# A feed-forward layer computed in two phases, most of its matrix products in two by two blocks with seven block products in place of eight

## The chip, the core and the metric

The kernel runs on one core of a Trainium2 chip. Its engines are TensorE (PE, matrix products into the accumulation memory PSUM), VectorE (DVE), ScalarE (ACT), GpSimd (POOL) and SyncE (SP), whose queue here issues every transfer between the device memory and the on-chip memory SBUF. Each engine works through its own list of instructions in order and waits at an instruction until what it needs is there. The metric is the device time of one execution in microseconds (us).

## The reference

One layer of a streaming encoder on 1024 new frames and 32 frames of a running stream, together T = 1056 rows of width D = 1024, all in float32. What matters here is the end of the layer, the feed-forward part:

```
mix = einsum(g_conv * y_conv + g_attn * y_attn, w_o)
x1  = layer_norm(ALPHA * x + mix)                         # LN1
h   = square(relu(einsum('btd,df->btf', x1, w_up)))       # 1024 -> 4096
out = layer_norm(ALPHA * x1 + einsum('btf,fd->btd', h, w_down))   # 4096 -> 1024, LN2
```

Before it stand an input projection, a convolution branch and an attention branch; the change does not touch them. The outputs also hold the keys, values and gate logs, which are unaffected.

## The kernel before

**Number format.** Every float32 operand of a product is split into a high and a low part (`whi`, `wlo` of a weight, `x1_0h`, `x1_0l` of an activation), and a product is the sum of three passes: high by high, high by low, low by high. So one block of 128 inputs by 128 outputs by n rows is three matmuls, each with its own load of 128x128 weights and n columns that stream through. `mm3` writes these passes and `dense` runs them to the end. A split is a copy on ACT (the high part) and a subtraction on DVE or POOL (the low part).

**Tiling.** Activations lie transposed: 128 channels on the partitions, the 1056 rows along the free axis. The rows are cut into three chunks of 352. Weights come as tiles of 128 outputs by 1024 inputs through the class `Weights`: `load` fetches half a tile (256 KB) into one of four `raw` buffers, `split` makes the high and low parts in a ring of four (`RB`), `take` and `drop` hand them out. From line 724 on the low parts of the weights are made on POOL (`W.engine = "pool"`).

**Order.** PE, DVE, ACT and POOL run exactly in the order in which the kernel's code records instructions; the class `Issue` records them and keeps a rough clock for each engine to decide when a background piece (a weight split, a step of a normalisation) is put in between. SP's order is set by the framework's scheduler.

**Merge, output projection, LN1.** The merge (`ps_yc`, `ps_yo`) works on 24 pieces of 128 channels by 352 rows. Then, chunk after chunk, `ps_o` is formed with `w_o` and added to the input into `acc` (eight tiles of 128x1056); `norm_out` runs LN1 as a background piece, whose `emit` writes the split `x1` tiles that the feed-forward part reads, and leaves `x1` itself in `acc`.

**Feed-forward.** An outer loop over eight blocks `fb` of four tiles of 128 hidden channels (`FB` = 4, `NFB` = 8). In each block `up` forms four tiles of hidden channels (8 input tiles x 3 passes = 24 matmuls of 352 columns for each tile and chunk); ACT takes the relu out of PSUM, DVE squares it (`r`), copies the high part (`hh`) and subtracts (`hl`). Then `down` forms the partial sums of eight output tiles (12 matmuls for each tile and chunk), and DVE adds each to `acc`. Hidden tiles never leave SBUF. In the last block the rows are handled in three pieces so that LN2 of an earlier piece runs beside the products of a later one; the end is written out by hand after LN2 of the last piece.

## Time and profile before

| | |
|---|---|
| Median of three runs | 1547.46 us (1547.21 to 1547.95) |
| Profiled execution, its own time | 1548.1 us |
| Its span from first to last instruction | 1546.3 us |
| Granted TensorE clock, mean | 0.988 |
| PE busy | 1501.4 us, 9524 matmuls |
| DVE, ACT, POOL busy | 900.7, 500.8, 466.5 us |
| Bytes moved | 165.57 MB, 107 GB/s over the span |
| Merge and output projection | about 600 to 773 us |
| Feed-forward with LN2 | about 773 us to the end |

How to read it: a group's row gives the source line (that of a helper such as `mm`, L205), the engine, the operation, the tile written and the tiles read, the shape and the count, then busy time, the mean duration of one instruction in ns, and the idle time of its engine just before, with what ended it. A matmul's own duration is much longer than its share of time, because matmuls overlap; the distance from one start to the next is what counts. A row of a stretch gives its length, each engine's busy time and (x count), the granted clock of TensorE (1.00 is full), the busy share of the 16 transfer engines and the rate in GB/s.

### The profile page before, as it was taken

The page shows a single profiled execution, that of the slowest core. Times are in us where ns is not written, and L with a number is a line of the kernel's source. Part 1 is how long each engine was busy: PE and PEld are TensorE (multiplying, and loading weights), DVE is VectorE, ACT ScalarE, POOL GpSimd, SP SyncE. Part 2 cuts the span into 40 slices and gives each one's busy share as a digit, 9 for nine tenths or more (in the row PEclk, how much of TensorE's full clock was granted, in tenths as well). Part 3 has the DMA queues.
Part 4 walks back from the last instruction along what each step waited for, and adds up shares of the span by engine and source line. Part 5 has one row for each costly group of instructions (what it writes and reads, how often), then busy time and mean ns, then how long its engine had stood idle before and what let it go on. Part 6 is the DMA issues. An engine that isn't in the chain of part 4 may idle for free.

```text
span 1546.3 us, 24721 instructions
## 1 busy us (share of the span) xinstructions
PE 1501.4 (97%) x9524; PEld 1473.8 (95%) x9524; DVE 900.7 (58%) x1461; ACT 500.8 (32%) x1086; POOL 466.5 (30%) x439
## 2 busy tenths in 40 slices
PE   9999999989999999999899999999999999999985
PEld 8999999989999998999899999999999999999984
DVE  6999899746666656748784342433334243342587
ACT  5123432536555564236541111211111021111133
POOL 0000000003454534567844222222222122231346
PEclk9999999999999999999999999999999999999998
DMA  6125453376445666544412111111111111114312
GB/s 232 43 77 160 165 175 126 131 215 168 134 129 169 171 225 207 153 139 146 142 42 81 42 42 55 42 42 55 42 42 55 42 42 55 42 59 146 137 38 75
DMA packets 114115, 165.57 MB, mean 107 GB/s; under 512 B 19530, under 2 KB 72010, under 8 KB 113998
## 3 DMA queue, kind: packets, MB, share of 16 engines
q1 hardware_dynamic: 113998, 163.99, 34.4%
q8 instruction: 75, 1.23, 0.3%
q14 instruction: 42, 0.34, 0.1%
HBM read 120.38 MB, written 43.54 MB: 106 GB/s over the span
## 4 chain that ended last, share of the span: by engine, by line
PE 83%; DVE 8%; DMA 3%; issue 2%; ACT 2%; SPq 1%; POOL 1%; ACTq 0%; DVEq 0%; POOLq 0%
PE ps_dn L205 22%; PE ps_up L205 22%; PE ps_g L205 9%; PE ps_v L205 3%; PE ps_glub L205 3%; PE ps_k L205 3%; PE ps_glua L205 3%; PE ps_q L205 3%; PE ps_o L205 2%; PE ps_s L205 2%; PE ps_pv L205 2%; PE ps_yc L205 2%; PE ps_tr L209 2%; DVE acc L234 2%; PE ps_yo L205 2%
## 5 line engine op out<-in xcount | busy, mean ns | idle before, releaser
L226 POOL TENSOR_TENSOR wlo<-raw,whi 128x512 fp32r<-128x512 f32 x204 | 285.6, 1421 | 542.4 <-ACT whi L217 541.3
L217 ACT ACTIVATE whi<-raw 128x512 fp32r<-128x512 f32 (+1 forms) x264 | 152.0, 623 | 405.4 <-issue 317.7
L205 PE MATMUL ps_dn<-hh,whi 128*128 128x352 f32 x768 | 249.4, 325 | 0.0
L205 PE MATMUL ps_dn<-hl,whi 128*128 128x352 f32 x768 | 247.8, 323 | 0.8 <-DVE hl L226 0.8
L205 PE MATMUL ps_dn<-hh,wlo 128*128 128x352 f32 x768 | 248.0, 323 | 0.0
L226 DVE TENSOR_TENSOR acc<-ps_dn,acc 128x352 f32<-128x352 f32 x168 | 87.8, 523 | 194.5 <-PE ps_dn L205 194.5
L234 DVE SCALAR_TENSOR_TENSOR ca<-u,prm,ca 128x1086 f32<-128x1086 f32 x120 | 161.7, 1348 | 2.4
L226 DVE TENSOR_TENSOR r<-r 128x352 f32<-128x352 f32 x96 | 52.5, 547 | 184.7 <-ACT r L217 184.7
L205 PEld LDWEIGHTS ps_dn<-hl,whi 128*128 128x128 f32 x768 | 144.5, 188 | 1.3 <-DVE hl L226 1.0
L205 PEld LDWEIGHTS ps_dn<-hh,whi 128*128 128x128 f32 x768 | 144.3, 188 | 0.6 <-DVE acc L226 0.2
L205 PEld LDWEIGHTS ps_dn<-hh,wlo 128*128 128x128 f32 x768 | 144.4, 188 | 0.0
L205 PE MATMUL ps_g<-xh,whi 128*128 128x352 f32 x384 | 132.4, 345 | 6.3 <-ACT gt L217 6.3
L217 ACT ACTIVATE r<-ps_up 128x352 f32<-128x352 f32 x96 | 44.5, 464 | 260.0 <-PE ps_up L205 253.5
L205 PE MATMUL ps_g<-xh,wlo 128*128 128x352 f32 x384 | 124.1, 323 | 0.0
L205 PE MATMUL ps_g<-xl,whi 128*128 128x352 f32 x384 | 122.0, 323 | 0.0
L226 DVE TENSOR_TENSOR hl<-r,hh 128x352 fp32r<-128x352 f32 x96 | 84.8, 883 | 3.3
L226 DVE TENSOR_TENSOR tl<-ps_tr,th 128x512 fp32r<-128x512 f32 (+2 forms) x96 | 51.2, 553 | 58.3 <-ACT th L217 57.5
L205 PE MATMUL ps_up<-x_0h,whi 128*128 128x352 f32 x256 | 82.9, 324 | 0.0
L205 PE MATMUL ps_up<-x_1h,wlo 128*128 128x352 f32 x256 | 82.4, 322 | 0.0
L205 PE MATMUL ps_up<-x_0h,wlo 128*128 128x352 f32 x256 | 82.4, 322 | 0.0
L205 PE MATMUL ps_up<-x_1h,whi 128*128 128x352 f32 x256 | 82.4, 322 | 0.0
L205 PE MATMUL ps_up<-x_0l,whi 128*128 128x352 f32 x256 | 82.3, 322 | 0.0
(281 smaller groups left out, 3774.9 us busy)
## 6 DMA issues: line engine op xcount, KB each, us to landing
raw<-in_w_in_dram SPq DMA_DIRECT2D x64, 256.0 KB
raw<-in_w_up_dram SPq DMA_DIRECT2D x64, 256.0 KB
raw<-in_w_down_dram SPq DMA_DIRECT2D x64, 256.0 KB
raw<-in_w_o_dram SPq DMA_DIRECT2D x48, 256.0 KB
g_s<-gt SPq DMA_DIRECT2D x48, 176.0 KB
yg<-g_s SPq DMA_DIRECT2D x48, 176.0 KB
xr<-in_x_dram SPq DMA_DIRECT2D x12, 352.0 KB
xr<-in_x_dram SPq DMA_DIRECT2D x24, 176.0 KB
```

The source lines that it names most:

```text
L205: self.nc.tensor.matmul(ps, lhsT=w, rhs=x, start=start, stop=stop)
L209: self.nc.tensor.transpose(ps, x, ident)
L217: self.nc.scalar.activation(out, in_, func, **kw)
L226: (self.nc.vector if eng == "dve" else self.nc.gpsimd).tensor_tensor(out, a, b, op)
L234: self.nc.vector.scalar_tensor_tensor(out, a, s, b, op0, op1)
```

## The change

The feed-forward part is done in two phases. First all hidden tiles are formed, then all outputs.

- **Blocks.** The rows are cut into four blocks of `CB` = 264. Both phases see their two factors as two by two blocks: rows in two halves, inputs in two halves, outputs in two halves. Seven products of sums of blocks give what eight products of blocks would give. In the first phase this is done for 14 of 16 pairs of hidden tiles (`NPL` = 2 pairs are done plainly), in the second for `NKB` = 6 of 8 blocks of hidden channels. The merge, the output projection and LN1 also use the four blocks of 264 rows.
- **Sums of weights.** The new class `Sums` loads four blocks of 128x512 of a unit, forms four sums (`s1` to `s4`) and splits seven operands, all sums and low parts on DVE.
- **Sums of x1.** `combine` forms the differences of the `x1` blocks and splits them (`th`, `tl`), once, between LN1 and the first of the seven-product pairs.
- **First phase.** For each pair of tiles `go(0)` to `go(6)` form seven products of 24 matmuls in a pair of PSUM banks (four such pairs). DVE adds them into `r11`, `r12`, `r22`, `r21` (128x528), ACT takes relu and square. `operands` then forms four sums and difference tiles of them and splits seven operands of the second phase (`parts_of`: high part on ACT, low part on DVE, three buffers `sp0` to `sp6` in turn), and each is written to device memory (`h_s`, 0.54 MB). `operands` of one pair is recorded among the products of the next; what is left of it at `go(4)` is recorded there in one piece (`I.finish`).
- **Second phase.** `load_h` reads the operands back (1.08 MB each, twelve buffers), seven products for each half of the outputs go into `acc2` and `aux`; `combined` and `residual` add up at the end. The last two blocks of hidden channels (`hp_s`) are done plainly with three pieces of 352 rows, beside LN2.

The core of the diff:

```diff
@@ constants @@
-HB = 5
-UPS = {0: ((0, CH), (CH, 2 * CH)), 2: ((2 * CH, T),)}
+CB = T // 4
+NB = 4
+GROUPS = ((0, 2), (1,), (3,))
+ORDER = (0, 2, 1, 3)
+NPL = 2
+NKB = 6
@@ class Sums, one unit u @@
+    self.split(block(0))
+    self.split(block(2))
+    s1 = total("s1", block(1), block(3), ADD)
+    s2 = total("s2", s1, block(0), SUB)
+    self.split(s2)
+    self.split(s1)
+    s3 = total("s3", block(0), block(1), SUB)
+    self.split(s3)
+    s4 = total("s4", block(2), s2, SUB)
+    self.split(s4)
+    self.split(block(3))
...
+        def split(self, raw):
...
+            act(hi, raw, AF.Copy)
+            tt(lo, raw, f32(hi), SUB)
@@ first phase @@
+        def parts_of(r, name, order="p s h x -> p h s x"):
+            sp = ph.tile([P, 2, 2, CB], F32R, tag="sp", bufs=3, name=name)
+            hi, lo = (sp.rearrange(order)[:, i] for i in range(2))
+            act(hi, r, AF.Copy)
+            tt(lo, r, f32(hi), SUB)
+            return sp
+        def operands(name, rs, dst):
...
+            out(0, r11)
+            out(5, r22)
+            tt(t3, r22, r12, SUB)
+            yield lag
+            out(4, t3)
+            tt(r12, r12, r11, SUB)
+            out(3, r12)
+            tt(r22, r22, r12, SUB)
+            out(2, r22)
+            out(1, r21)
+            tt(r21, r21, r22, SUB)
+            out(6, r21)
...
+    def product(name, terms):
+        ps = pair_bank(name)
+        for s, half in enumerate(terms):
+            out = ps[:, s, :CB]
+            for n, (wh, wl, h, l) in enumerate(half):
+                mm(out, wh, h, n == 0, False)
+                mm(out, wh, l, False, False)
+                mm(out, wl, h, False, n == len(half) - 1)
...
+        for p in range(NPL, D_FF // P // 2):
+            act(r21, go(0), AF.Copy)
+            tt(r11, r21, go(1), ADD)
+            square(r11)
+            tt(r21, r21, go(2), ADD)
+            tt(r12, r21, go(3), ADD)
+            ps = go(4)
+            if streams:
+                I.finish(streams[-1])
+            tt(r22, r12, ps, ADD)
+            tt(r21, r21, ps, ADD)
+            square(r22)
+            tt(r12, r12, go(5), ADD)
+            square(r12)
+            tt(r21, r21, go(6), ADD)
+            square(r21)
@@ second phase @@
+            for kb in range(NKB):
+                for g in range(2):
+                    for i in range(7):
...
+                        for n in range(2):
+                            ps = product(f"d{i}", ...)
+                            if kb == 0:
+                                act(v, ps, AF.Copy)
+                            else:
+                                tt(v, ps, v, ADD)
```

What this does to the order on the engines is seen at three places. In the feed-forward part before, DVE has for each tile and chunk one square and one split, of 352 columns:

```order
L226 TENSOR_TENSOR acc7_8061<-ps_dn_180_11558,acc7_8061 128x352
L226 TENSOR_TENSOR r3_0_0_11609<-r3_0_0_11609 128x352
L221 CAST hh12_11582<-r3_0_0_11609 128x352
L226 TENSOR_TENSOR hl12_11583<-r3_0_0_11609,hh12_11582 128x352
L226 TENSOR_TENSOR r3_0_352_11636<-r3_0_352_11636 128x352
```

Now, in the middle of the ninth pair, DVE goes from the sum with product 3 of this pair through what was left of the operands of pair 8 (sums `r12`, `r22`, `r21` and splits `sp4` to `sp6`) to the sums with product 4, then on to the weights of the next unit (`s3`, `s4` and their low parts `swlo30`):

```order
L230 TENSOR_TENSOR sp4_8_12509<-t3_8_12404,sp4_8_12509 128x2x264
L230 TENSOR_TENSOR r12_8_12177<-r12_8_12177,r11_8_12112 128x528
L230 TENSOR_TENSOR sp3_8_12514<-r12_8_12177,sp3_8_12514 128x2x264
L230 TENSOR_TENSOR r22_8_12274<-r22_8_12274,r12_8_12177 128x528
L230 TENSOR_TENSOR sp2_8_12519<-r22_8_12274,sp2_8_12519 128x2x264
L230 TENSOR_TENSOR sp1_8_12523<-r21_8_12073,sp1_8_12523 128x2x264
L230 TENSOR_TENSOR r21_8_12073<-r21_8_12073,r22_8_12274 128x528
L230 TENSOR_TENSOR sp6_8_12528<-r21_8_12073,sp6_8_12528 128x2x264
L230 TENSOR_TENSOR r22_9_12532<-r12_9_12441,ps_u4_166_12484 128x528
L230 TENSOR_TENSOR r21_9_12343<-r21_9_12343,ps_u4_166_12484 128x528
L230 TENSOR_TENSOR swlo30_12538<-s3_8_12459,swhi30_12537 128x512
L230 TENSOR_TENSOR s4_8_12541<-sraw34_12231,s2_8_12451 128x512
```

Several of these rows read what the row ahead of them wrote, after a pass through ACT. ACT's rows of the same place make the high parts, and the relu and square (x2) of `r22`, `r12`, `r21` stand between them:

```order
L221 ACTIVATE sp3_8_12514<-r12_8_12177 128x2x264
L221 ACTIVATE sp2_8_12519<-r22_8_12274 128x2x264
L221 ACTIVATE sp1_8_12523<-r21_8_12073 128x2x264
L221 ACTIVATE sp6_8_12528<-r21_8_12073 128x2x264
L221 ACTIVATE r22_9_12532<-r22_9_12532 128x528 x2
L221 ACTIVATE swhi30_12537<-s3_8_12459 128x512
L221 ACTIVATE swhi30_12537<-s4_8_12541 128x512
L221 ACTIVATE r12_9_12441<-r12_9_12441 128x528 x2
L221 ACTIVATE r21_9_12343<-r21_9_12343 128x528 x2
L221 ACTIVATE swhi31_12604<-sraw35_12313 128x512
```

So a high part of the next weights (`swhi30`, `swhi31`) comes after the relu and square of this pair. The third place is the seam in front of the first such pair. On DVE the last rows of `combine` (the low parts `tl2`, `tl4` of the differences of x1) stand ahead of the first low part of the weights, `swlo0`, which the first product `ps_u0` needs:

```order
L230 TENSOR_TENSOR d2_3_10433<-acc7_8373,d2_3_10433 128x528
L230 TENSOR_TENSOR tl2_0_10270<-d2_3_10433,th7_10436 128x264
L230 TENSOR_TENSOR tl2_1_10271<-d2_3_10433,th7_10436 128x264
L230 TENSOR_TENSOR tl4_0_10276<-d2_3_10433,th7_10436 128x264
L230 TENSOR_TENSOR tl4_1_10277<-d2_3_10433,th7_10436 128x264
L230 TENSOR_TENSOR swlo0_10453<-sraw0_9761,swhi0_10452 128x512
```

Before, DVE had nothing of this kind between LN1 and the feed-forward products. In all PE's 4608 feed-forward matmuls of 352 columns become 4752 of 264 (384 plain, 2352 in the first phase, 2016 in the second) and 576 of 352, and 1080 of 352 columns in the merge and the output projection become 1440 of 264.

774 lines of the change are left out of this document (514 added, 260 removed).

## The prediction

> **What bounds the kernel now.** I read the busy table first, then the chain of waits, then stretches of the feed-forward part.
>
> ```profile
> span 1546.3 us, 24721 instructions
> PE 1501.4 (97%) x9524; PEld 1473.8 (95%) x9524; DVE 900.7 (58%) x1461; ACT 500.8 (32%) x1086; POOL 466.5 (30%) x439
> 960.66 46.01 PE ps_up L205 x288
> 1006.67 46.44 PE ps_dn L205 x288
> 1100.00:1200.00 100.00, 100.00 (x626) 100.00 (x625) 37.24 (x67) 15.13 (x30) 25.26 (x18) 1.00 0.16 48
> ```
>
> In the chain PE follows PE: 288 matmuls of 352 columns in 46.01 us (up), then 288 in 46.44 us (down), which is 159.8 and 161.3 ns from start to start. In the stretch below them PE is busy all the time, DVE for 37% and the transfer engines for 16%. So PE bounds this part, and streaming fewer columns is worth its full time until another engine becomes the bound. The profiled execution took 1548.1 us, 0.6 above the median; the sum is made against it.
>
> **What the change takes off PE.** The row nearest to 264 columns is that of the value projection:
>
> ```profile
> L205 PE MATMUL ps_v<-whi,xh x144: 277/282/292, 102.3 to 153.6; 128*128 128x260 f32 x144
> L205 PE MATMUL ps_v<-whi,xl x144: 277/283/288, 102.5 to 153.8; 128*128 128x260 f32 x144
> ```
>
> Three such kinds take turns: 432 matmuls, the first at 102.3, the last at 153.8 us, so 119.5 ns each. On the line from there to 352 columns, 264 costs 121.3 ns. Feed-forward before: 2304 x 159.8 + 2304 x 161.3 ns = 740 us. Now: 4752 x 121.3 + 576 x 161.3 ns = 669 us. That is -70.5 us; merge and output projection (1080 x 159.8 ns against 1440 x 121.3 ns) give 2 back. **Term: -68.4.** One seven-product pair is 168 x 121.3 ns = 20.4 us on PE.
>
> **What it puts on DVE.** Each pair has seven sums out of PSUM, four sums and seven low parts for the operands (18 of 528 columns), and four sums and seven low parts for the next weights (11 of 512).
>
> ```profile
> 20.41 2.69 DVE L226 TENSOR_TENSOR xl<-xr,xh 128x352 fp32r<-128x352 f32 x6
> 34.07 1.29 DVE L226 TENSOR_TENSOR wlo<-raw,whi 128x512 fp32r<-128x512 f32 x2
> L226 DVE TENSOR_TENSOR xl<-xr,xh x24: 512/518/526, 5.5 to 22.6; 128x352 fp32r<-128x352 f32 x24
> L226 DVE TENSOR_TENSOR wlo<-raw,whi x60: 673/686/701, 4.7 to 321.5; 128x512 fp32r<-128x512 f32 x52, 128x520 fp32r<-128x520 f32 x8
> ```
>
> Back to back, six of 352 take 2.69 us with one lasting 0.52, so they stand 0.434 apart; two of 512 take 1.29 with 0.686 each, so 0.604 apart. At 528 columns I take 0.62 apart and an end 0.70 after the start. A pair is then 18 x 0.62 + 11 x 0.60 = 17.8 us, below PE's 20.4. If nothing else counted, PE would stay the bound.
>
> But DVE does not run these back to back. In the fenced order of the ninth pair a low part reads a sum that DVE wrote one row earlier, after ACT has copied its high part in between. The price of such a round trip:
>
> ```profile
> L217 ACT ACTIVATE whi<-raw x264: 613/622/641, 4.0 to 1454.1; 128x512 fp32r<-128x512 f32 x128, 128x520 fp32r<-128x520 f32 x4
> 747.06 0.51 DVE L226 TENSOR_TENSOR acc<-acc,ps_mu_n 128x352 f32<-128x352 f32 x1
> 747.66 0.50 ACT L217 ACTIVATE lnsq_n<-acc 128x352 f32<-128x352 f32 x1 [0.37 <-DVE acc L226]
> 906.62 0.47 ACT L217 ACTIVATE r<-ps_up 128x352 f32<-128x352 f32 x1 [2.34 <-PE ps_up L205]
> 907.11 0.53 DVE L226 TENSOR_TENSOR r<-r 128x352 f32<-128x352 f32 x1 [1.42 <-ACT r L217]
> L226 DVE TENSOR_TENSOR tl<-ps_tr,th 128x512 fp32r<-128x512 f32 (+2 forms) x96 | 51.2, 553 | 58.3 <-ACT th L217 57.5
> ```
>
> ACT begins 0.09 us after DVE's end (747.57 to 747.66), DVE 0.02 after ACT's (907.09 to 907.11). ACT needs 0.622 for 512 columns, 0.64 for 528. So the low part starts 0.70 + 0.09 + 0.64 + 0.02 = 1.45 us after its sum did, instead of 0.62: 0.83 lost each time. The last row shows that this happens: the transposed tiles have the same pair of steps with nothing between, and DVE waited 57.5 us for ACT in 96 of them, 0.6 each.
>
> Going down both orders row by row, a pair has five such round trips (4.2 us): `s2`, `r12` to `sp3`, `r22` to `sp2`, `r21` to `sp6`, `s4`. Beside them come high parts that stand on ACT behind the relu and square of a tile that DVE has just summed. In the ninth pair `swlo30` waits for two passes over `r22` and its own copy (1.4 us), `swlo31` for four passes over `r12` and `r21` and its copy (2.65). That is 4.0 us. The pairs of even number, where the planner puts the weights elsewhere, have three such places: a copy behind four passes (2.9), and two behind one tile's passes each, just after its sum (2.05 each), 7.0 us in all. Odd pairs have 28 DVE rows, 17.2 us, and come to 17.2 + 4.2 + 4.0 = 25.4; even pairs have 30, 18.4 us, and come to 18.4 + 4.2 + 7.0 = 29.6; the mean is 27.6. The four pair banks let PE run three products (8.7 us) ahead of DVE: that evens out one wait, but not a mean over eleven pairs. **Term: 11 full pairs x (27.6 - 20.4) = +79**, and +3 for pairs 13 to 15, whose operands are lighter. The bounds: zero if DVE and ACT always find other work done, and +150 if the writes join in (below).
>
> **The seam before the first such pair.**
>
> ```profile
> 772.34 0.33 PE L205 MATMUL ps_o<-m2h,wlo 128*128 128x352 f32 x1
> 790.00:800.00 10.00, 10.00 (x64) 10.00 (x63) 9.76 (x16) 5.22 (x11) 4.46 (x4) 1.00 0.01 2
> 800.00:810.00 10.00, 10.00 (x65) 10.00 (x64) 9.40 (x15) 5.62 (x11) 4.13 (x4) 1.00 0.00 0
> 340.00:350.00 10.00, 8.43 (x45) 7.80 (x46) 4.43 (x14) 4.88 (x14) 2.51 (x2) 0.74 0.75 215
> ```
>
> After the output projection (772.3 us) DVE is still nearly full with LN1 between 790 and 810 us, some 20 to 25 us of work. Now follow the plain pairs' operands (15 rows of about 0.62, 9 us) and `combine` (16 differences of 528 columns at 0.62 and 32 low parts of 264 at 0.35, by the line through the two widths above, 21 us, and some 3 of waits for ACT's high parts: 24), and only then `swlo0`, for which `ps_u0` waits. That is about 59 us against 384 x 121.3 ns = 46.6 us of plain products: **+13** (3 to 25). After such a stall the clock is low, as in the row at 340 us (granted 0.74, 45 matmuls in 8.43 busy us, 7.2 at the full rate): **+1**. The Trainium skill ("TensorE: Matmul & The Clock Gate", "Part 1: The HAM clock gate") has half the clock after an idle window of some 3.4 us until as much busy time has passed. The row agrees that the clock drops; by the rule the estimate would be 1.7 in place of 1.
>
> **The second phase.** Its half block has 25 DVE rows, 15.4 us, and some 2.5 of waits, 17.9 against 20.4 on PE: PE bounds it. It reads 9.7 MB for each block of hidden channels in 40.8 us, 237 GB/s.
>
> ```profile
> 410.00:420.00 10.00, 8.66 (x62) 8.46 (x63) 6.96 (x14) 7.11 (x15) 6.54 (x9) 1.00 0.81 226
> 570.00:580.00 10.00, 10.00 (x74) 9.58 (x73) 5.98 (x12) 7.26 (x17) 2.21 (x4) 1.00 0.97 342
> 1450.00:1460.00 10.00, 10.00 (x65) 10.00 (x64) 5.11 (x9) 1.50 (x3) 3.02 (x2) 1.00 0.94 351
> 573.39 9.84 DMA o_s<-oh
> ```
>
> Stretches moved 342 and 351 GB/s, so it fits, with a third to spare. The first weight block of this phase stands on SP's queue behind twelve operand loads (13 MB / 350 GB/s = 37 us, part of it beside the last pairs): **+8** for this seam (0 to 25).
>
> **The tail.** Beside LN2, PE has gaps:
>
> ```profile
> 1480.00:1490.00 10.00, 9.66 (x56) 8.80 (x55) 9.21 (x14) 2.82 (x5) 4.47 (x4) 1.00 0.07 25
> 1490.00:1500.00 10.00, 9.09 (x58) 8.80 (x56) 9.69 (x14) 5.06 (x13) 7.56 (x7) 1.00 0.34 121
> 1500.00:1510.00 10.00, 7.12 (x34) 6.62 (x35) 8.74 (x14) 2.76 (x6) 2.52 (x3) 0.83 0.00 0
> 1510.00:1520.00 10.00, 9.25 (x55) 8.66 (x54) 8.18 (x11) 4.00 (x7) 6.08 (x6) 1.00 0.42 146
> 1520.00:1530.00 10.00, 5.97 (x35) 5.18 (x33) 9.51 (x17) 2.98 (x6) 7.34 (x7) 0.99 0.00 0
> ```
>
> These 50 us hold 238 matmuls where a full stretch (at 790 us) holds 64 in 10 us, 320: 82 x 160 ns = 13 us are lost. With 24 matmuls for each tile in place of 12, DVE has half the sums for the same PE work: **-9** (0 to -13).
>
> **Sum:** -68.4 + 79 + 3 + 13 + 1 + 8 - 9 = +26.6; 1548.1 + 26.6 = 1574.7, less the 0.6 of the profiled execution: **1574 us**. Without the pairs' term (and its 3) the rest is -55.4; so the change breaks even at a pair time of 20.4 + 52.4/11 = 25.2 us.
>
> **The rivals.**
>
> - *PE stays the bound in the pairs (faster).* The banks, and rows that find ACT already done, hide the round trips. For it: DVE's own 17.8 us are below 20.4. Against it: the order has no independent row between sum and low part, and the 57.5 us above were not hidden. 1548.1 - 55.4 - 0.6 = **1492**. It decides below 25.2 us a pair; with half the waits (DVE 22.7, still above PE) the time is about 1520.
> - *The writes come late (slower still).* Three `sp` buffers serve seven operands a pair, so a high part waits for the write of the operand three before. If a write lands 9.84 us after its issue, as the row of `o_s` shows, seven operands through three buffers take 7/3 x (9.84 + 1.45) = 26 us; sums and weight rows that stand in line behind them bring a pair to about 34, and the time to 1574 + 6.5 x 11 = **1646**. Against it: in the rows at 1450 and 570 us the transfers move far more than the pairs' 3.8 MB per 27 us.
> - *Reading back bounds the second phase.* At 200 GB/s, below the 226 of the stretch at 410 us, a block takes 48.4 us instead of 40.8: six times 7.6 on top, **1620**.
>
> **How the numbers follow.** Chances: forecast 0.57, with a range of its own from 1540 to 1610 (pairs of 24.5 to 31 us); PE-bound pairs 0.28; late writes 0.09; reading back 0.06. A difference under 0.2% (3 us) can hardly be told from none. Faster: 0.28, and 0.08 of the forecast's own lower end, 0.36; same 0.03; slower 0.61. The range is 1485 to 1625: it leaves out the late writes and the edge of the PE-bound case.
>
> **What would show it.** Right: in the first phase PE busy for about three quarters of the stretches, `ps_u` starts 121 ns apart within a product, DVE's idle time ahead of `sp` and `swlo` rows ended by ACT, that of the `ps_u` matmuls by DVE; about 17.8 us of DVE work in 27 to 28 us a pair; a stall of some 13 us before `ps_u0`, ended by DVE; the second phase full at about 41 us a block; fewer gaps in the tail. Wrong: stretches of the pairs with PE full, or a time below 1540, mean that the round trips were hidden; idle time of ACT or DVE ended by transfers at `sp` speaks for late writes; `ps_d` ended by loads for reading back.

## The result, and the profile after

The changed kernel takes **1629.07 us** (median of four runs, 1628.7 to 1631.47) against 1547.7 us before, a ratio of 1.0529 with a 95% interval of 1.051 to 1.0547. It is 81 us slower. The prediction said slower, 1574 us, with a range of 1485 to 1625: the direction and the mechanism of the seven-product pairs came out, the size did not, and 1629 lies outside the range.

The first view is the page of the changed kernel, its span and busy times:

```profile
span 1626.9 us, 28163 instructions
PE 1472.6 (91%) x10608; PEld 1440.5 (89%) x10608; DVE 1157.6 (71%) x1843; ACT 684.0 (42%) x1409; POOL 315.2 (19%) x346
```

The profiled execution took 1628.7 us, 80.6 more than that of the kernel before. PE is idle for 154 us of the span, where it was idle for 45 before. The borders of the stages come from the rows of single tiles (duration min/median/max in ns, then the first and the last start):

```profile
L209 PE MATMUL ps_up<-x_0h,whi x32: 280/284/795, 783.8 to 801.3; 128*128 128x264 f32 x32
L209 PE MATMUL ps_up<-x_3h,wlo x32: 279/284/290, 826.6 to 837.9; 128*128 128x264 f32 x32
L209 PE MATMUL ps_u<-x_0h,swhi x112: 280/287/589, 861.4 to 1223.3; 128*128 128x264 f32 x112
L209 PE MATMUL ps_d<-hu,swhi x1344: 280/284/589, 1240.9 to 1510.1; 128*128 128x264 f32 x192
L209 PE MATMUL ps_dn<-hs,whi x384: 318/323/592, 1510.4 to 1610.0; 128*128 128x352 f32 x192
```

With these borders the difference of 80.6 us splits as follows. Each stage's loss is its length less its matmuls at 121.3 ns (161.3 ns for the 352 columns of the tail).

| Stage | from, to (us) | predicted term | measured |
|---|---|---|---|
| matmul time of the feed-forward part | | -70.5 | -70.5 (taken at the same ns) |
| merge, output projection | to 783.8 (772.5 before) | +2 | +11.3 |
| plain pairs and the stall behind them | 783.8, 861.4 | +13 | 77.6 - 46.6 = +31.0 |
| fourteen seven-product pairs | 861.4, 1240.9 | +79 +3 +1 | 379.5 - 285.6 = +93.9 |
| second phase | 1240.9, 1510.4 | +8 | 269.5 - 244.5 = +25.0 |
| tail with LN2 | 1510.4, 1626.9 | -9 | 116.5 - 92.9 - 33.8 = -10.2 |

The last row compares with the 33.8 us that the whole feed-forward part lost before (773.8 us of it, 740 of matmuls). The fourth row takes a pair at 20.4 us. The terms that were too small add 9.3, 18, 11 and 17 us, the tail gives 1 back: 54 us between forecast and result.

In the pairs the profile looks as the forecast said. In the middle of this stage (columns: length, busy time and count of PE, weight loads, DVE, ACT, POOL, then granted clock, transfer share and GB/s):

```profile
900.00:1160.00 260.00, 210.97 (x1558) 208.89 (x1557) 172.20 (x265) 125.26 (x213) 0.00 (x0) 0.88 0.46 171
```

and, from the timeline of ACT:

```profile
899.78 0.59 ACT L221 ACTIVATE r<-ps_u 128x528 f32<-128x528 f32 x1
1155.98 0.59 ACT L221 ACTIVATE r<-ps_u 128x528 f32<-128x528 f32 x1
```

These rows are ACT's copy of the first product of a pair; nine pairs lie between them, 256.2 us, so a pair takes 28.5 us (27.6 to 29.1; the expectations below say 29.0, the longer of two neighbours). PE runs 1558 matmuls, 189 us of work at full rate (121.3 ns each), in 260 us. DVE is not full either (172 us). What they wait for shows in the waits between 870 and 1240 us (total, times, longest):

```profile
DVE swlo L230 <- ACT swhi L221: 71.6, 61, 2.5
DVE sp L230 <- ACT sp L221: 41.0, 50, 2.3
ACT r L221 <- DVE r L230: 62.4, 40, 2.9
ACT swhi L221 <- DVE s L230: 55.9, 27, 4.1
ACT sp L221 <- DVE r L230: 52.1, 29, 2.8
ACT sp L221 <- DMA h_s<-sp: 11.0, 11, 3.1
PE ps_u L209 <- ACT r L221: 62.9, 11, 9.1
```

DVE waits for ACT and ACT waits for DVE, in the same stage, and neither waits for PE. PE waits for them, once or so in a pair and up to 9.1 us. Rows of DVE and ACT, in order of time, show the round trip itself:

```profile
1000.10 0.70 DVE L230 TENSOR_TENSOR r<-r,r 128x528 f32<-128x528 f32 x1
1000.83 0.64 ACT L221 ACTIVATE sp<-r 128x528 fp32r<-128x528 f32 x1 [1.40 <-DVE r L230]
1001.51 0.71 DVE L230 TENSOR_TENSOR sp<-r,sp 128x528 fp32r<-128x528 f32 x1 [0.71 <-ACT sp L221]
1002.44 0.64 ACT L221 ACTIVATE sp<-r 128x528 fp32r<-128x528 f32 x1 [0.97 <-DMA h_s<-sp]
1003.12 0.71 DVE L230 TENSOR_TENSOR sp<-r,sp 128x528 fp32r<-128x528 f32 x1 [0.90 <-ACT sp L221]
```

A sum starts at 1000.10, its low part at 1001.51: 1.41 us, where the forecast had 1.45. The next copy (1002.44) waited for something that the sum left out, a buffer that is still being written to memory. The chain of waits has that write:

```profile
998.17 4.18 DMA h_s<-sp
```

It takes 4.18 us from its issue, and ACT waited 0.97 us for it.

### The profile page after: what moved, and what is told of

Same layout as the page of the kernel before. It is cut to its first block, busy times and chain, and to the rows that moved or that the text cites. A ratio compares the mean times of both kernels' runs of the same rounds, so it can differ in the third digit from the quotient of the medians.

```text
span 1626.9 us, 28163 instructions
## 1 busy us (share of the span) xinstructions
PE 1472.6 (91%) x10608; PEld 1440.5 (89%) x10608; DVE 1157.6 (71%) x1843; ACT 684.0 (42%) x1409; POOL 315.2 (19%) x346
## 4 chain that ended last, share of the span: by engine, by line
PE 55%; DVE 19%; ACT 11%; DMA 7%; issue 5%; SPq 1%; POOL 1%; DVEq 0%; ACTq 0%; POOLq 0%
PE ps_d L209 12%; PE ps_g L209 11%; ACT r L221 4%; PE ps_v L209 3%; PE ps_o L209 3%; DVE r L230 3%; PE ps_k L209 3%; PE ps_glua L209 3%; PE ps_glub L209 3%; PE ps_q L209 3%; DVE s L230 3%; PE ps_dn L209 3%; ACT swhi L221 3%; DVE swlo L230 3%; DMA h_s<-sp 3%
## 5 line engine op out<-in xcount | busy, mean ns | idle before, releaser
L230 POOL TENSOR_TENSOR wlo<-raw,whi 128x512 fp32r<-128x512 f32 x100 | 138.9, 1410 | 753.4 <-ACT whi L221 753.4
L209 PE MATMUL ps_d<-hu,swhi 128*128 128x264 f32 x1344 | 249.6, 286 | 19.2 <-ACT aux L221 6.0
L209 PEld LDWEIGHTS ps_d<-hu,swhi 128*128 128x128 f32 x1344 | 210.9, 190 | 20.9 <-issue 7.3
L209 PE MATMUL ps_d<-hu,swlo 128*128 128x264 f32 x672 | 193.1, 287 | 0.2 <-DVE swlo L230 0.2
L209 PE MATMUL ps_u<-th,swhi 128*128 128x264 f32 x448 | 128.3, 286 | 0.0
L209 PEld LDWEIGHTS ps_d<-hu,swlo 128*128 128x128 f32 x672 | 127.7, 190 | 0.4 <-DVE swlo L230 0.4
L209 PE MATMUL ps_u<-tl,swhi 128*128 128x264 f32 x448 | 127.8, 285 | 0.0
L209 PE MATMUL ps_u<-th,swlo 128*128 128x264 f32 x448 | 127.7, 285 | 0.0
L221 ACT ACTIVATE r<-r 128x528 f32<-128x528 f32 (+1 forms) x128 | 77.6, 616 | 68.9 <-DVE r L230 66.6
L209 PE MATMUL ps_dn<-hs,whi 128*128 128x352 f32 x384 | 94.3, 327 | 1.0 <-DVE acc L230 1.0
L209 PEld LDWEIGHTS ps_u<-th,swhi 128*128 128x128 f32 x448 | 85.3, 190 | 0.4 <-issue 0.2
```

Of the source, the lines that this page charges most:

```text
L209: self.nc.tensor.matmul(ps, lhsT=w, rhs=x, start=start, stop=stop)
L221: self.nc.scalar.activation(out, in_, func, **kw)
L230: (self.nc.vector if eng == "dve" else self.nc.gpsimd).tensor_tensor(out, a, b, op)
```

## The experiments

A pair's time is read as above, from the first products' copies between 900 and 1160 us (for the kernels with the plain first phase from the first start of the fourteen pairs to the first start of the second phase; for e8 and e10 without pair 13, whose operands are lighter). Beside these runs the kernel before took 1547.1 to 1548.4 us, so they can be compared with one another to about 1 us.

| Run | what is different | us | pair, us |
|---|---|---|---|
| the change | | 1629.1 | 28.5 |
| e1_low_pool | low parts of the pairs' weights on POOL | 1579.7 | 23.9 |
| e2_weights_pool | and the sums of weights on POOL | 1674.9 | 31.5 |
| e3_loads | fewer operand loads ahead in phase two | 1629.1 | as the change |
| e4_reorder | sums of the operands first | 1639.9 | 29.3 |
| e5_pipe | another row between high and low part | 1628.9 | 28.6 |
| e6_buffers | e4 with four buffers | 1622.2 | 27.7 |
| e7_combine | half of the x1 differences' low parts on POOL | 1633.0 | as the change |
| e8_all | e1, e5, e7, four buffers, weights earlier | 1570.8 | 23.8 |
| e9_high_dve | all high parts of the pairs on DVE | 1596.6 | 25.6 |
| e9b_operands_dve | those of the operands only | 1630.2 | 28.2 |
| e10_mix | e1, e9b, four buffers, earlier weights | 1568.4 | 24.0 |
| e11_plain_up | first phase without seven products | 1548.2 | 23.2 |
| e12_plain_ring | e11 with seven buffers | 1541.7 | 23.2 |
| e13_plain_ring_loads | e12 and e3 | 1540.9 | 23.2 |

### Is it the order of DVE and ACT that sets a pair?

**Less for DVE to do.** e1 moves seven rows of a pair to POOL:

```diff
@@ Sums.split @@
-            tt(lo, raw, f32(hi), SUB)
+            tt(lo, raw, f32(hi), SUB, "pool" if n < 7 * (16 - NPL) else "dve")
```

> Only change: in the fourteen seven-product pairs the seven low parts of the weights (swlo) are made on POOL, not on DVE. Theory (DVE's order with its waits for ACT sets the pair): each full pair loses seven rows of 0.60 us and the waits in front of them (71.6 us over the fourteen pairs, 5.1 each), so it goes from 29.0 us to 20 to 24 us, 24 if DVE's rows get longer while POOL works on the same memory; swlo0 no longer stands behind the x1 differences, so the first two products start some 20 us earlier and the seam loses about 6 us; total 1540 to 1580 us. Rival (the writes to memory bind the three buffers): the pairs stay at 27 us or more and the waits of the copies for the writes grow from 11 us to over 40; total above 1610. Rival (the lower granted clock of TensorE costs the time by itself): the pairs keep a granted clock below 0.9 and stay above 25 us.

Measured: 1579.69 us, 49 less, pairs of 23.9 us, both at the upper edge of what the theory gave; the granted clock rose to 0.95 (second of the two stretches below). One part did not come: `ps_u0` was no earlier (864.3 us against 861.4) and waited for `swhi0`, whose copy stands behind the x1 differences on ACT (the last two of their passes start at 862.55, `swhi0` at 863.64), as its low part did on DVE. By itself this run does not separate DVE's waits from its amount of work, since both shrink.

**More moved, and slower.** e2 moves the sums `s1` to `s4` as well:

```diff
@@ Sums.steps, total @@
-                    tt(t, a, b, op)
+                    tt(t, a, b, op, "pool" if u < 16 - NPL else "dve")
```

> As the kernel with the low parts on POOL, and the four sums of weights of each pair on POOL too, so that DVE has 18 rows in a pair (11.2 us) and POOL 11 (15.5 us at the 1.41 us that the kernel before shows for one). Theory: DVE's order no longer binds; a pair is PE's 20.4 us, or POOL's 15.5 plus some 5 us of waits for ACT, 21 to 22; total 1530 to 1560 us, not above the run with the low parts alone by more than 10. Rival (writes): pairs stay above 27 us.

Measured: 1674.92 us, 95 more than e1, though DVE had the least to do of all the kernels with seven-product pairs (123.6 us in 900 to 1160 us). Its waits between 870 and 1240 us:

```profile
ACT swhi L221 <- POOL s L230: 72.5, 26, 4.9
DVE sp L230 <- ACT sp L221: 163.1, 70, 9.6
```

Now three engines wait in a ring. A sum takes 1.3 us and more on POOL, ACT waits for it with the high part, and everything behind that high part on ACT waits too, the operands' copies among it; DVE then waits for those, 163.1 us in place of 41.0 in the change and 63.1 in e1. The expectation had added up POOL's own work and missed who stands behind ACT. The rival's sign (pairs above 27 us) came too, but ACT's waits for the writes are only 24.2 us here. Again it is the order, not an engine's amount of work, that decides.

**More for DVE to do, but no hand-over.** e9 is the counter-test: it gives DVE all fourteen copies of the high parts.

```diff
@@ parts_of, and in the same way Sums.split for the pairs @@
-            act(hi, r, AF.Copy)
+            cp(hi, r)
             tt(lo, r, f32(hi), SUB)
```

> Only change: in the seven-product pairs the fourteen high parts (seven of operands, seven of weights) are copied on DVE, not on ACT. DVE gets more work: fourteen copies of about 0.42 us by the line through 0.288 us for 264 and 0.344 us for 352 columns, 5.8 us on top of 17.8 us, 23.6 us a pair; but no low part waits for ACT any more. If the waits between the two engines set the pair: 29.0 us falls to 23.6 to 25 us, total 1565 to 1590 us. If DVE's amount of work set it: the pair grows to 33 us or more, total above 1670. If the writes to memory set it: within 10 of 1629.

Measured: 1596.58 us, 32 less, pairs of 25.6 us. The stretches of e9, and below it of e1, for 900 to 1160 us:

```profile
900.00:1160.00 260.00, 224.43 (x1721) 221.55 (x1720) 248.74 (x440) 56.93 (x92) 0.00 (x0) 0.93 0.52 193
```

```profile
900.00:1160.00 260.00, 238.06 (x1863) 235.83 (x1862) 186.59 (x238) 146.42 (x255) 114.88 (x80) 0.95 0.55 203
```

DVE is busy for 248.74 of 260 us in e9, against 172.20 in the changed kernel, and more products come out. So the waits between the two engines set the pair, and not DVE's work: DVE is busy for 77 us more of this stretch, and each pair is 3 us shorter. The total lies 7 us above the expected range and the pair 0.6 us, as DVE had 24.5 us a pair to do where 23.6 was worked out; with 24.5 of 25.6 us DVE itself is now the bound.

**Half of it gives nothing.** e9b has the edit in `parts_of` alone, so that only the operands' high parts are made on DVE.

> As the kernel with all high parts on DVE, for the operands alone: the weights keep their high parts on ACT. DVE 17.8 + 2.9 = 20.7 us a pair, and the waits of swlo for ACT (5.1 us a pair) stay or shrink, as ACT has seven passes less. Waits theory: pair 24.5 to 26.5 us, total 1590 to 1612 us, between the kernel of the change and the run with all high parts on DVE. If the waits only move to the weights, as they did when the splits were taken apart: pair 28 us or more, total above 1620.

Measured: 1630.15 us, no change; the expectation of a gain fell, and the other case named with it came (pairs of 28.2 us). Its waits:

```profile
DVE swlo L230 <- ACT swhi L221: 79.4, 62, 2.5
DVE sp L225 <- DMA h_s<-sp: 1.3, 1, 1.3
```

The 41.0 us of waits for the operands' copies are gone, 2.9 us a pair, and seven copies of 0.43 us, 3.0 us a pair, stand in their place. The waits of the weights did not shrink with ACT's load: the relu and square that stand ahead of `swhi` in ACT's order, as worked out for `swlo30` and `swlo31`, are the likely reason, which no run tested by itself.

### Round trips or buffers: which is next?

e4 forms the sums `t3`, `r12`, `r22` one behind the other, ahead of the splits:

```diff
@@ operands @@
             tt(t3, r22, r12, SUB)
-            yield lag
-            out(4, t3)
             tt(r12, r12, r11, SUB)
-            yield lag
-            out(3, r12)
             tt(r22, r22, r12, SUB)
             yield lag
+            out(4, t3)
+            out(3, r12)
             out(2, r22)
             yield [r21]
+            tt(t3, r21, r22, SUB)
             out(1, r21)
-            yield lag
-            tt(r21, r21, r22, SUB)
-            out(6, r21)
+            out(6, t3)
```

> Only change: in the operands of a pair the three sums t3, r12, r22 are formed one behind the other and only then copied and split (and the last difference goes to t3), so a low part no longer stands right behind its own sum. Theory (round trips of 0.83 us each): two to three of five go, a pair loses 1.7 to 2.5 us, eleven pairs 19 to 27, total 1602 to 1612 us. Rival (writes): the copies now follow each other faster than their three buffers are written out, the waits for the writes grow from 1 us to 3 us or more a pair and take the gain; total 1625 to 1640 us.

e5 leaves the sums where they are and puts one other DVE row between the high and the low part of most splits, of weights and operands:

```diff
@@ Sums.split @@
             act(hi, raw, AF.Copy)
-            tt(lo, raw, f32(hi), SUB)
+            self.settle()
+            self.open.append((len(self.parts), lo, raw, hi, freed))
@@ operands @@
-            out(4, t3)
+            o4 = out(4, t3)
             tt(r12, r12, r11, SUB)
+            o4()
...
```

> Only change: every split is taken apart in the order, so that between the high part on ACT and the low part on DVE one other DVE row (the next sum, or the next split's work) stands; same instructions, same engines, three buffers. Theory (round trips and copies that stand behind relu and square set the pair): in the operands 0.62 of each 0.83 us is covered, about 2 us a pair, and the waits of swlo (71.6 us over the pairs) fall to about half; a pair goes from 29.0 to 24 to 26 us, total 1575 to 1600 us. Rival (the three buffers wait for the writes): as in the run with the sums first, the waits for the writes grow above 30 us and the total stays above 1615.

Measured: e4 1639.87 us, 11 more; e5 1628.9 us, unchanged. Both expectations of a gain fell, and the rival named with them came in its place (in e5 with waits of 29.1 us, just under the 30 that it named). ACT's waits for the writes, 11.0 us in the changed kernel, are in e4 and in e5:

```profile
ACT sp L221 <- DMA h_s<-sp: 49.8, 10, 6.5
```

```profile
ACT sp L221 <- DMA h_s<-sp: 29.1, 19, 3.6
DVE swlo L230 <- ACT swhi L221: 71.2, 47, 2.9
```

The operands come in a burst at `go(4)`. When their copies follow each other faster, the three buffers are still on their way to memory. In e5 the row put between high and low part also left the waits of the weights as they were (71.2 us), since these come from what stands ahead on ACT and not from the neighbouring row.

e6 gives e4 a fourth buffer, paid with one of LN1's:

```diff
-            sp = ph.tile([P, 2, 2, CB], F32R, tag="sp", bufs=3, name=name)
+            sp = ph.tile([P, 2, 2, CB], F32R, tag="sp", bufs=4, name=name)
-        rstd = tmp("lnrstd", 2, f"rstd_{tag}")[:, :n]
+        rstd = tmp("lnrstd", 1 if LNW == CB else 2, f"rstd_{tag}")[:, :n]
```

> The kernel with the sums first (1639.9 us), and four buffers in place of three for the operands on their way to memory (one buffer of LN1's is given up for it). If the waits for the writes (49.8 us in the pairs there) took the gain of the order: they fall below 20 us, a pair loses 2 to 3 us, total 1605 to 1620 us. If they did not, and the bunching of the sums itself costs the time: total stays within 5 of 1640.

Measured: 1622.22 us, pairs of 27.7 us, 18 less than e4 and 7 less than the change. The buffer helps, as said; but the waits for the writes fell only to 43.7 us and not below 20, so this row does not account for a pair that is 1.6 us shorter. DVE's waits for the operands' copies fell by more, from 49.0 us in e4 to 34.6, or 1.3 us for each of the eleven full pairs. No run has the fourth buffer in the order of the change.

### The seam and the start of the second phase

e7 makes every second low part of `combine` on POOL, which is idle there.

```diff
@@ combine, put @@
-                            tt(tl[i][s][:, k, :], t[:, half], f32(th[m][:, cs])[:, half], SUB)
+                            tt(tl[i][s][:, k, :], t[:, half], f32(th[m][:, cs])[:, half], SUB, "pool" if s else "dve")
```

> Only change: half of the low parts of the x1 differences (16 of 32 rows) are made on POOL, which is idle there. Theory (DVE's own rows set the end of that stage and so the start of the first seven-product pair): the differences take 18 to 22 us in place of 28, the stall before ps_u0 goes from 23 to 14 to 18 us, total 6 to 10 us less, 1619 to 1623. Rival (POOL and DVE hinder each other on SBUF, as rows of 1.79 us in place of 0.70 in the run with the low parts on POOL suggest): no gain, within 3 of 1629.

Measured: 1632.95 us, 4 us more and no gain. The differences take as long as before. DVE's groups between 826 and 866 us are, in e7:

```profile
L230 DVE TENSOR_TENSOR tl<-d,th 128x264 fp32r<-128x264 f32 x16 | 9.8, 613 | 6.7 <-ACT th L221 5.9
L230 DVE TENSOR_TENSOR d<-acc,d 128x528 f32<-128x528 f32 x8 | 7.8, 976 | 0.1
```

and in the changed kernel (to 863 us):

```profile
L230 DVE TENSOR_TENSOR tl<-d,th 128x264 fp32r<-128x264 f32 x32 | 11.7, 429 | 5.9 <-ACT th L221 5.9
L230 DVE TENSOR_TENSOR d<-acc,d 128x528 f32<-128x528 f32 x8 | 5.6, 704 | 0.1
```

Half of the rows are gone, and the rest grew from 429 to 613 ns and from 704 to 976 ns: what POOL took off, it cost DVE again. The 5.9 us of waits for ACT stayed. The rival held, with a loss of 4 us where it had named up to 3.

e3 changes the loads at the start of the second phase:

```diff
-                        while ahead < min(7 * kb + 12 + i * g, 7 * NKB):
+                        while ahead < min(7 * kb + 12 + i * g, 7 * NKB, 5 + i if kb + g == 0 else 99):
```

> Only change: at the start of the second phase at most five operands (and one more per product) are loaded ahead of the first weights, in place of twelve. Theory (the first weight blocks stand behind twelve operand loads on SP's queue): DVE's wait of 21.9 us for the weights shrinks below 5, PE's idle time between 1240 and 1330 us goes from about 17 us to 3 to 8, total 10 to 15 us less, 1614 to 1619 us; the pairs unchanged. Rival (the memory's rate binds there in any case, 403 GB/s between 1260 and 1280 us): PE then waits for the operands instead, total within 4 us of 1629.

Measured: 1629.11 us, unchanged. DVE's wait of 21.9 us for the first weights did go and PE was full from 1260 to 1310 us. Then e3 has

```profile
1310.00:1320.00 10.00, 8.21 (x68) 7.99 (x66) 6.34 (x11) 2.64 (x5) 0.00 (x0) 1.00 0.17 55
1320.00:1330.00 10.00, 8.13 (x45) 8.17 (x46) 9.17 (x14) 1.45 (x3) 0.00 (x0) 0.66 0.59 194
```

Here 113 matmuls stand where 165 fit, 6 us, with DVE late on the next weights; the changed kernel lost its time between 1270 and 1290 us. The gain was given back 40 us later. The rival's total came, but not its cause: PE's longest wait of this stretch, 3.66 us at 1321.87 us, ends by a sum on DVE and not by a load of operands.

### Undoing one half of the change

e8 and e10 put the parts together that shorten a pair. New in them are the first two weight blocks split ahead of the x1 differences,

```diff
@@ Sums.ahead @@
-                if not self.next or not self.pool:
+                if not self.next or not (self.pool or len(self.parts) < 2):
```

and in e10 the low parts of the differences, which are recorded one step later (the same rows in another order).

> Together: splits taken apart in the order, low parts of the pairs' weights on POOL, four buffers for the operands, half of the low parts of the x1 differences on POOL, and the first two weight blocks split ahead of the x1 differences. Theory: DVE's order no longer sets the pair, which comes to 20.4 to 22 us (PE), the stall before ps_u0 vanishes for the first two products and a shorter one of 5 to 10 us stands before the third; total 1520 to 1550 us. If the writes or TensorE's clock set the pair: 23 us or more, total above 1560.

> Together: high parts of the operands on DVE, low parts of the pairs' weights on POOL, four buffers for the operands, the first two weight blocks split ahead of the x1 differences, and the differences with their low parts one step later in the order. DVE has 18 x 0.62 + 4 x 0.60 + 7 x 0.42 = 16.5 us a pair and some 3 us more from rows that grow longer while POOL works (as in the run with the low parts on POOL). Theory: PE sets the pair, 20.4 to 21.5 us; the differences take 22 us in place of 28; total 1520 to 1545 us. If waits stay at 23 us a pair: 1555 to 1565 us.

Measured: 1570.8 us (ratio 1.0149, 1.0131 to 1.0167) and 1568.36 us (1.0132, 1.0115 to 1.0149), pairs of 23.8 and 24.0 us. Both are better than the change by some 60 us, both slower than before, and neither pair reached PE's 20.4 us. For e8 the rival's figures came (23 us or more, above 1560), but not its two causes: between 870 and 1140 us no wait of ACT or DVE ends by a write of `h_s`, and the granted clock is 0.99. There DVE still waits 39.5 us for ACT's copies, and its `sp` rows take 1095 ns on the mean. The stall of e8 only moved: its first two products run at once, and 23.47 us stand before the third, where 5 to 10 were expected. In e10 it fell apart into waits of 5.4, 6.2 and 5.8 us between 838 and 885 us. DVE is full in e10 (251.2 of 260 us), for another reason than in e9:

```profile
L230 DVE TENSOR_TENSOR sp<-r,sp 128x528 fp32r<-128x528 f32 x57 | 68.9, 1208 | 2.0
```

These rows take 1208 ns on the mean, and 708 in the changed kernel (the last section says why). A plain pair costs PE 192 x 0.1213 = 23.3 us. So the seven products of the first phase, at 23.8 us, no longer save anything, and still bring the x1 differences and the waits before the first products.

e11 therefore forms all pairs plainly and keeps seven products in the second phase:

```diff
-    plan += [io["w_up"][f] for f in range(2 * NPL)]
+    plan += [io["w_up"][f] for f in range(D_FF // P)]
...
-                        I.add(combine(), "combine")
...
         for p in range(NPL, D_FF // P // 2):
+            rs = []
+            for i in range(2):
+                wh, wl = W.take()
+                for t in range(2):
+                    if i and t and streams:
+                        I.finish(streams[-1])
+                    ps = product(f"u{2 * i + t}", [[(col(wh, k), col(wl, k), xt[2 * t + s][0][:, k, :], xt[2 * t + s][1][:, k, :])
+                                                   for k in range(KD)] for s in range(2)])
+                    r = hidden(f"r{i}{t}_{p}")
+                    act(r, ps, AF.Relu)
+                    act(r, r, AF.Square)
+                    rs.append(r)
+                W.drop()
+            r11, r12, r21, r22 = rs
```

> One half of the change undone: all sixteen pairs of the first phase are formed plainly (192 matmuls of 264 columns a pair, weights split as in the merge, low parts on POOL), with the same operands written to memory; the second phase keeps its seven products. The sums of weights, the sums out of PSUM and the x1 differences of the first phase fall away: DVE has eleven rows a pair. Theory: PE is the bound again, a pair takes 192 x 0.1213 = 23.3 us (the pairs of the change took 27.1 on the mean, 29.0 where they are full), no stall of 23 us stands behind the plain pairs, so the second phase starts at 838 + 14 x 23.3 = 1164 us in place of 1241; its own start loses less, as the last pair leaves less to drain: total 1540 to 1553 us. If the stage was slow for another reason (blocks of 264 columns, the writes, the clock): the pairs stay above 26 us, total above 1590.

Measured: 1548.15 us, a ratio of 1.0002 (0.9993 to 1.0011) to the kernel before: the whole loss of 81 us is gone, as expected (the second phase starts at 1163.4 us, where 1164 was worked out). Its stretch, and the start of its second phase:

```profile
900.00:1160.00 260.00, 260.00 (x2153) 260.00 (x2152) 86.52 (x111) 119.98 (x206) 55.55 (x40) 1.00 0.53 194
```

```profile
L209 PE MATMUL ps_d<-hu,swhi x1344: 280/284/589, 1163.4 to 1429.1; 128*128 128x264 f32 x192
```

PE is full at a clock of 1.00 with the same blocks of 264 columns and the same writes, so these by themselves do not slow the stage: between 850 and 1160 us ACT waits 26.5 us for the writes of `sp`, more than the 11.0 us in the change, and PE does not notice. More matmuls (2688 for the fourteen pairs in place of 2352) take less time: 325 us from 838.3 on, in place of 379.5 from 861.4. The operands alone (11 DVE rows a pair) hide under PE.

Two more runs ask where the second phase loses its 25 us. e12 lets the operands use seven buffers, the three of before and four of the rows that held x1 differences; e13 adds the edit of e3.

```diff
@@ parts_of @@
-            sp = ph.tile([P, 2, 2, CB], F32R, tag="sp", bufs=3, name=name)
+            nsp[0] += 1
+            if nsp[0] % 7 < 3:
+                sp = ph.tile([P, 2, 2, CB], F32R, tag="sp", bufs=3, name=name)
+            else:
+                sp = row(9 + nsp[0] % 7, name).rearrange("p (s h x) -> p s h x", s=2, h=2)
```

> The kernel with the plain first phase, and seven buffers in place of three for the operands on their way to memory (four rows of x1 differences that this kernel does not use). If the copies of the last pair that wait for their writes cause the loss at the start of the second phase: the wait of 4.2 us on ACT and the 3.5 us of PE go, and some 2 us of low clock with them, total 1540 to 1545 us. If the weights' place on the queue causes it: the loss moves to the wait for the weights (14.7 us on DVE), total within 2 of 1548.

> As the kernel with seven buffers, and at most five operands (and one more per product) loaded ahead of the first weights of the second phase. If both causes act one after the other: the second phase takes 250 to 256 us from its first to its last seven-product matmul in place of 266, total 1532 to 1540 us. If the loads' order only moves the loss, as in the kernel of the change: total as in the run with seven buffers alone, within 2 us.

Measured: 1541.65 us (ratio 0.9958, 0.9946 to 0.997) and 1540.88 us (0.9948, 0.9934 to 0.9962). Their second phases, e12 and e13:

```profile
L209 PE MATMUL ps_d<-hu,swhi x1344: 280/283/587, 1165.1 to 1426.8; 128*128 128x264 f32 x192
```

```profile
L209 PE MATMUL ps_d<-hu,swhi x1344: 280/284/558, 1161.9 to 1421.1; 128*128 128x264 f32 x192
```

It takes 265.7 us in e11, 261.7 in e12 and 259.2 in e13. With the buffers 4 us of it go, and 6.5 us of the median time (the two profiled executions lie 2.3 apart). ACT's wait of 4.2 us and PE's of 3.5 are gone, as expected of the first cause; but PE now waits 4.1 us for a high part of weights, so part of the loss moved to the weights, as the other cause has it. The loads' order adds 2.5 us in these profiles, but the times of the two lie within each other's spread (1540.57 to 1544.49, and 1536.48 to 1542.1), so that it adds anything is not shown: the 250 to 256 us expected of e13 did not come, its second case (within 2 us of e12) did. Of the 259.2 us of e13 some 15 are still lost, about half of them before 1260 us. Both kernels are faster than the kernel before, by 0.4 to 0.5%: with seven products in the second phase alone the change pays, and just.

## Why the prediction was right or wrong

**What bounds before, and the matmul time: right.** 264 columns cost 120.9 ns in e11 (2688 in 325.1 us), where the line gave 121.3.

**The pairs: right in kind, 11 us short.** The term was +79 with 3 and 1 beside it; measured are 93.9. The round trip was 1.41 us against 1.45, the pair 28.5 against 27.6 us. e9 shows that waits and not work set it, e1 and e2 that their order does. Almost all of the shortfall lies in the eleven full pairs: 28.5 us on the mean give 11 x (28.5 - 20.4) = 89 where the term had 79. It lies in the odd ones: 25.4 us were worked out for them and 27.6 to 29.1 came, while the even ones, worked out at 29.6, took 28.7 to 29.1. One thing that the step left out are the writes: it used their row only for a rival with 9.84 us and left out the shorter wait that the three buffers bring. ACT's waits for them are 11.0 us over the pairs, and they stand close behind the round trips, as e4 and e5 show. That this is as much as the shortfall does not make it the cause: such waits of about 1 us stand in the even pairs too, and how much of the 11 us they make stays open. The rival of late writes in its own form (pairs of 34 us) did not come. PE as the bound of the pairs did not come either, except in e11, where the pairs' products are plain.

**The seam before the first pair: wrong in size, the first of two steps that take the time out of its range.** "+13 (3 to 25)" was 31.0. The stall itself and the stretch around it:

```profile
861.44 0.59 PE L209 MATMUL ps_u<-x_0h,swhi 128*128 128x264 f32 x1 [23.28 <-ACT swhi L221]
```

```profile
834.00:862.00 28.00, 4.72 (x37) 4.45 (x35) 21.95 (x49) 12.36 (x24) 0.00 (x0) 0.66 0.07 28
```

Two terms of this step were too small. `combine` was put at 24 us and took 28: it starts behind the last split of the plain pairs at 833.7 and ends at 861.75 us, with low parts 0.35 us apart as worked out, but a wait of 0.71 to 0.76 us before each of eight groups (5.9 us where 3 were allowed for). And LN1 was given 20 to 25 us after the output projection, from a stretch of the kernel before; here it ran until 823 us, 39 after it, and the plain pairs' operands waited for ACT (up to 3.04 us for one low part). The stretch was also read wrongly: of the 19 us of DVE's work between 790 and 810 us only 5 are rows of LN1, the rest are hidden tiles (`r`, `hh`, `hl`), and LN1's last row there ended at 804.2 us, 32 after the output projection. The stall ended by ACT and not by DVE as forecast: `swhi0` starts at 860.77 us on ACT and `swlo0` at 861.75 on DVE, each right behind the last of the differences. The clock after it cost more than the 1 us that the sum had (last section).

**Merge and output projection: a term that was not made.** The step counted only matmuls, "+2", and 11.3 were measured. The merge's first matmul came 1.3 us later already (561.1 against 559.8), the merge took 114.3 us in place of 109.2, and the output projection 108.4 in place of 103.5 (675.4 to 783.8, against 669.0 to 772.5). PE's longest waits there are, before:

```profile
750.55 1.54 PE L205 MATMUL ps_var_n<-lnvar_n,mean_d 128*128 128x352 f32 x2 [5.44 <-DVE lnvar_n L226]
```

and after:

```profile
595.65 0.39 PE L209 MATMUL ps_yo<-yol,whi 128*128 128x264 f32 x1 [2.30 <-DMA yol<-o_s]
757.28 1.25 PE L209 MATMUL ps_mu_n<-lnsum_n,mean_d 128*128 128x264 f32 x2 [3.65 <-DVE lnsum_n L230]
781.42 0.59 PE L209 MATMUL ps_o<-m3h,wlo 128*128 128x264 f32 x1 [2.42 <-POOL wlo L230]
```

The wait in the merge is for a load. In the output projection LN1 runs beside PE, as before, and PE's waits there come to 8.7 us in place of 6.3. Four blocks of 264 rows give LN1 a third more instructions than three of 352, and a row does not get shorter by the same share: DVE's scaling of `acc` is 32 rows of 942 ns there and was 24 of 1082 ns. I cut the reference's end into blocks of another size and priced it for PE alone. That the larger count is the cause is argued from these rows and no run changed it; e11, e12 and e13 carry the loss too (782.2, 786.9 and 784.3 us to the first plain pair, against 772.5).

**The second phase: wrong in size, the second of the two.** "+8 (0 to 25)" was 25.0, at the upper bound. The step saw the weights behind the operand loads, and had about their price: between 1270 and 1290 us, where DVE's wait of 21.9 us for them ends, 112 matmuls stand where 165 fit, 6 us. It did not see that the last pair has to be drained first: the copies that free the accumulation banks stand on ACT behind the last pair's splits, and these wait for their writes (2.91 us for the last one, at 1253.86 us). Two stretches of the changed kernel:

```profile
1240.00:1250.00 10.00, 6.29 (x48) 5.97 (x48) 5.38 (x10) 5.56 (x10) 0.00 (x0) 1.00 0.87 311
1250.00:1260.00 10.00, 3.96 (x21) 3.91 (x21) 4.47 (x7) 5.76 (x11) 0.00 (x0) 0.66 0.92 322
```

69 matmuls stand where 165 fit: 11 to 12 us, the larger part of what the step missed. e12 takes the buffers' part of it away, e3 and e13 show that the loads' order moves the rest more than it removes it. From 1320 to 1490 us PE runs at 84 matmuls in 10 us but for 1350 to 1370 (152 in 20), and none of its waits in this phase ends by a load, so reading back does not bound it: that rival fell.

**The tail: near**, but not by the -10.2 of the table, which sets it against all that the feed-forward part lost before. From 1480 us on the kernel before had 222 feed-forward matmuls in 66.3 us, 30.6 lost; the tail now loses 23.6. That is -7 against -9; the other 3 us were lost before at the start of the part.

Taken together, the direction rests on the pairs' term, whose mechanism was right. The time left its range by four terms that were too small, the seam before the first pair (18 us short) and the start of the second phase (17 us short) above all.

## What to carry to other kernels

Where two engines run fixed orders and hand tiles to each other, add up the round trips and what stands ahead of each hand-over in the other's queue, and not each engine's busy time: DVE's 18.9 us of busy time (172.2 of 260 us) filled 28.5 us here, and in e9 24.5 us without these hand-overs filled 25.6. Ask the same of a cure, since the next wait (here the buffers on their way to memory, or a third engine in the ring) often stands right behind. And when an algorithm saves one matmul in eight, price the sums it adds, the drain at each new border between phases, and every other stage that its block size cuts anew; in this layer it paid only in the second phase, with the sums for its operands hidden under the plain products of the first.

## What the runs showed of the hardware

**POOL and DVE hinder each other, by what DVE reads.** In e1, with POOL's rows beside them (the first row is POOL's, two instructions that end at 1032.26 us):

```profile
1028.77 3.49 POOL L230 TENSOR_TENSOR swlo<-s,swhi 128x512 fp32r<-128x512 f32 x2
1029.30 1.79 DVE L230 TENSOR_TENSOR r<-r,r 128x528 f32<-128x528 f32 x1
1031.02 0.69 DVE L230 TENSOR_TENSOR r<-r,ps_u 128x528 f32<-128x528 f32 x1
```

A DVE row with both inputs in SBUF goes from 0.70 to 1.79 us while POOL works, and a row with one input in PSUM stays at 0.69. Over e1's pairs the `sp` rows take 911 ns on the mean, and the 96 sums out of PSUM between 690 and 705. The Trainium skill says this ("SBUF — State Buffer", "SBUF: two separate sides"): a DVE instruction with two SBUF inputs and a GpSimd instruction that reads SBUF share one pair of ports under an exclusive lock. The rows agree, and they give its price: in e1 the rows that moved to POOL were worth it, in a stage where DVE had waited anyway; in e7, where DVE was the bound, they were not, and in e10 DVE is full with rows that got longer. A copy with its one input in SBUF gets longer as well: the operands' CAST rows take 432 ns on the mean in e9, without POOL, and 687 in e10.

**The clock after a stall.** After the stall of 23.28 us the changed kernel has

```profile
862.00:867.00 5.00, 4.76 (x23) 4.51 (x22) 4.23 (x7) 1.16 (x3) 0.00 (x0) 0.53 0.00 0
```

The granted clock is 0.53, the matmuls start 0.22 us apart until 866.62 and 0.12 from 866.80 on, 5.4 us after the first one. Some 21 matmuls at this clock cost 21 x 0.10 = 2.1 us, where the sum had 1. The rule of the Trainium skill that the prediction named ("TensorE: Matmul & The Clock Gate", "Part 1: The HAM clock gate") agrees in kind and not in length: it has some 3.4 us, and its estimate was 1.7. After the stalls of e1 and e8 (23.3 and 23.5 us) the half rate lasted 6.8 and 7.1 us, with a wait of PE of 0.8 and 0.9 us behind the second matmul. In the pairs the mean granted clock was 0.88, and it rose as PE's waits fell (0.95 in e1, 1.00 in e11). That it cost time there by itself was not tested; between 870 and 1240 us none of the waits of DVE and ACT shown above ends by PE.
